# Dealing the tokens to the partitions in two groups, so that the rows of a transfer lie closer together in HBM

## The chip, the core and the metric

The kernel runs on one core of one Trainium2 chip; the other seven cores are idle. The metric is the device time of the whole program in microseconds. Before the change the median of 3 runs is 240.83 us (240.64 to 241.17). The profile is one more execution of the same program: 240.54 us by the clock that the metric uses, and a span of 238.8 us from the first to the last instruction in the trace.

## The reference

Each of 16 x 1024 = 16,384 tokens is a row of 512 float32 numbers (2 KB). It is written out twice, each time multiplied by one of its two weights. The expert indices are an input, but nothing is computed from them.

```python
def setup_inputs():
    batch, seq, hidden, n_experts = 16, 1024, 512, 8
    k = 2
    return {
        "x": np.random.randn(batch, seq, hidden).astype(np.float32),
        "expert_indices": ...,                      # not used
        "expert_weights": np.random.randn(batch, seq, k).astype(np.float32),
    }

def reference(x, expert_indices, expert_weights):
    x_expanded = x[:, :, np.newaxis, :].repeat(k, axis=2)
    weights = expert_weights[..., np.newaxis]
    return (x_expanded * weights).astype(np.float32)   # (16, 1024, 2, 512)
```

So 33.6 MB are read and 67.1 MB are written, for one multiplication per number written.

## The kernel before

Every partition of the on-chip memory gets 128 consecutive tokens (`A_TOTAL`): partition p has the tokens 128p to 128p + 127. One transfer moves, for each of the 128 partitions, one contiguous row of bytes; the rows of one transfer start 128 tokens apart in HBM, which is 256 KB in `x` and 512 KB in `out`.

```python
A_TOTAL = ntok // P                     # 16384 / 128 = 128 tokens per partition
xr = x.rearrange("b s h -> (b s) h").rearrange("(p a) h -> p (a h)", a=A_TOTAL)
outr = ...                              # the same for out, 1024 numbers per token
wr = ...                                # the same for the weights, 2 per token
row = k * hidden                        # 1024 numbers: both copies of a token
TX = 16                                 # tokens per partition in one load
TO = 8                                  # tokens per partition in one store
w_pool = ...(bufs=1); x_pool = ...(bufs=2); o_pool = ...(bufs=4)

w_tile = w_pool.tile([P, A_TOTAL * k], f32)
nc.sync.dma_start(out=w_tile, in_=wr)                       # all weights, once

for i in range(A_TOTAL // TX):                              # 8 loads
    x_tile = x_pool.tile([P, TX * hidden], f32)
    nc.scalar.dma_start(out=x_tile, in_=xr[:, i*TX*hidden : (i+1)*TX*hidden])
    for j in range(TX // TO):                               # 2 stores per load
        o_tile = o_pool.tile([P, TO * row], f32)
        for t in range(TO):
            for kk in range(k):
                nc.vector.tensor_scalar(                    # 128 x 512, times a weight
                    out=o_tile[:, o : o + hidden],
                    in0=x_tile[:, at : at + hidden],
                    scalar1=w_tile[:, c : c + 1], scalar2=None,
                    op0=mybir.AluOpType.mult)
        nc.sync.dma_start(out=outr[:, first : first + TO*row], in_=o_tile)
```

Loads are issued from ScalarE's queue, the weights and the stores from SyncE's queue. A load row is 16 tokens or 32 KB, a store row 8 tokens of two copies or 32 KB; so every load and every store moves 128 rows of 32 KB, 4 MB. There are two buffers for loads and four for stores.

Of the kernel before, what the change touches and what calls it, by code (L numbers as in the profile page):

```python
# [1 line left out]

# [4 lines left out]


@with_exitstack
def kernel(  # L10
    ctx: ExitStack,
    tc: tile.TileContext,
    x: bass.AP,
    expert_indices: bass.AP,
    expert_weights: bass.AP,
    out: bass.AP,
):
    nc = tc.nc

    batch, seq, hidden = x.shape  # L20
    k = expert_weights.shape[-1]
    P = nc.NUM_PARTITIONS
    ntok = batch * seq
    assert ntok % P == 0
    A_TOTAL = ntok // P

    xr = x.rearrange("b s h -> (b s) h").rearrange("(p a) h -> p (a h)", a=A_TOTAL)
    outr = out.rearrange("b s k h -> (b s) (k h)").rearrange(
        "(p a) n -> p (a n)", a=A_TOTAL
    )  # L30
    wr = expert_weights.rearrange("b s k -> (b s) k").rearrange(
        "(p a) k -> p (a k)", a=A_TOTAL
    )
    f32 = mybir.dt.float32
    row = k * hidden

    TX = 16
    TO = 8

    w_pool = ctx.enter_context(tc.tile_pool(name="w_pool", bufs=1))  # L40
    x_pool = ctx.enter_context(tc.tile_pool(name="x_pool", bufs=2))
    o_pool = ctx.enter_context(tc.tile_pool(name="o_pool", bufs=4))

    w_tile = w_pool.tile([P, A_TOTAL * k], f32)
    nc.sync.dma_start(out=w_tile, in_=wr)

    for i in range(A_TOTAL // TX):
        x_tile = x_pool.tile([P, TX * hidden], f32)
        nc.scalar.dma_start(
            out=x_tile, in_=xr[:, i * TX * hidden : (i + 1) * TX * hidden]  # L50
        )
        for j in range(TX // TO):
            o_tile = o_pool.tile([P, TO * row], f32)
            for t in range(TO):
                at = (j * TO + t) * hidden
                for kk in range(k):
                    c = (i * TX + j * TO + t) * k + kk
                    o = t * row + kk * hidden
                    nc.vector.tensor_scalar(  # L59
                        out=o_tile[:, o : o + hidden],  # L60
                        in0=x_tile[:, at : at + hidden],
                        scalar1=w_tile[:, c : c + 1],
                        scalar2=None,
                        op0=mybir.AluOpType.mult,
                    )
            first = (i * TX + j * TO) * row
            nc.sync.dma_start(out=outr[:, first : first + TO * row], in_=o_tile)


# [1 line left out]
_INS = ['x', 'expert_indices', 'expert_weights']  # L71
_OUTS = [((16, 1024, 2, 512), 'float32')]


# [23 lines left out]
```

## Time and profile before

| what | value |
|---|---|
| time, median of 3 | 240.83 us |
| span of the profiled execution | 238.8 us |
| HBM read and written in it | 33.69 MB and 67.11 MB |
| VectorE multiplications | 256, 102.5 us in all |
| loads of `x` | 8 of 4 MB |
| stores of `out` | 16 of 4 MB |
| load of the weights | 1 of 128 KB, landed 10.1 us after its issue |

To read such a profile: the core has 16 DMA engines, and every transfer is spread over them, row by row. "DMA share" is the mean busy share of the 16; a share slightly over 1 comes from packets being counted in the stretch in which they start. "Landing" is the moment when the semaphore of a transfer has its full count, so that an engine waiting for it can go on. "Idle before" of a group of instructions says how long their engine stood still ahead of them, and what ended it; that costs time only if the engine sets the pace.

### The profile page before, as it was taken

What the parts mean: (1) busy time and instruction counts of PE and PEld (TensorE: products, weight loads), DVE (VectorE), ACT (ScalarE), POOL (GpSimd) and SP (SyncE); (2) the same over time, 40 slices, a digit from 0 to 9 for tenths busy, and PEclk for the clock granted to TensorE, in tenths of its full rate; (3) what the DMA queues carried; (4) which work ended last, traced back from release to release, by engine and by line L of the source; (5) the groups of instructions that cost most, each with busy time, mean ns of one, the idle gap of its engine ahead of it and who ended that gap; (6) DMA issues with size and microseconds to landing.
All of it is one profiled execution on the core that took longest, in us unless ns stands there. A gap on an engine that the chain in (4) does not pass through costs nothing.

```text
span 238.8 us, 358 instructions
## 1 busy us (share of the span) xinstructions
DVE 102.5 (43%) x256; POOL 0.2 (0%) x4
## 2 busy tenths in 40 slices
DVE  0079994059701904682054910739008486400000
POOL 0000000000000000000000000000000000000000
DMA  7999999999999999999999999999999999999994
GB/s 277 447 439 417 434 380 417 439 439 439 423 423 428 439 423 412 439 439 439 439 439 434 434 439 439 412 435 428 428 423 434 434 439 439 439 439 434 434 439 214
DMA packets 3602, 100.81 MB, mean 422 GB/s; under 512 B 400, under 2 KB 528, under 8 KB 528
## 3 DMA queue, kind: packets, MB, share of 16 engines
q1 hardware_dynamic: 2448, 67.24, 65.4%
q10 hardware_dynamic: 1152, 33.55, 33.2%
q14 instruction: 2, 0.02, 0.0%
HBM read 33.69 MB, written 67.11 MB: 422 GB/s over the span
## 4 chain that ended last, share of the span: by engine, by line
DMA 62%; DVE 18%; another core or an unknown queue 5%; DVEq 0%; issue 0%
DMA out_dram<-o_tile 57%; DVE o_tile L59 18%; DMA x_tile<-in_x_dram 5%; DVEq L93 0%; DVEq L59 0%
## 5 line engine op out<-in xcount | busy, mean ns | idle before, releaser
L59 DVE TENSOR_SCALAR o_tile<-x_tile,w_tile 128x512 f32<-128x512 f32 x256 | 102.5, 480 | 103.3 <-DMA out_dram<-o_tile 74.1
L82 POOL MEMSET const-bfloat16-1.0<- 128x1 bf16 x1 | 0.1, 101 | 0.0
L82 POOL MEMSET const-uint8-127<- 128x1 uint8 x1 | 0.1, 101 | 0.0
L82 POOL MEMSET const-float32-0.0<- 128x1 f32 x1 | 0.1, 98 | 0.2 <-issue 0.2
L82 POOL MEMSET const-float32-1.0<- 128x1 f32 x1 | 0.1, 98 | 0.0
## 6 DMA issues: line engine op xcount, KB each, us to landing
out_dram<-o_tile SPq DMA_DIRECT2D x16, 4096.0 KB, 44.9
x_tile<-in_x_dram ACTq DMA_DIRECT2D x8, 4096.0 KB, 23.9
w_tile<-in_expert_weights_dram SPq DMA_DIRECT2D x1, 128.0 KB, 10.1
```

The lines of the kernel that those rows point to most:

```text
L59: nc.vector.tensor_scalar(out=o_tile[:, o : o + hidden], in0=x_tile[:, at : at + hidden], scalar1=w_tile[:, c : c + 1], scalar2=None, op0= ...
L82: nc = _bacc.Bacc("TRN2", target_bir_lowering=False, num_devices=1)
```

## The change

The tokens are dealt in two groups. The first group has 65 tokens per partition (tokens 0 to 8,319), the second 63 (the rest). In the first group the rows of a transfer start 65 tokens apart: 130 KB in `x`, 260 KB in `out`. In the second they start 63 tokens apart: 126 KB and 252 KB. The aim is that the rows which the DMA engines work on at the same moment do not all lie at a multiple of 256 KB from one another.

As 65 and 63 don't divide by 16, the loads have other sizes: five loads of 13 tokens (26 KB per row) in the first group, and loads of 16, 16, 16 and 15 tokens in the second. Stores still take at most 8 tokens. A load of 13 tokens is stored as 8 and 5 (rows of 32 and 20 KB), the load of 15 as 8 and 7. The weights come by two transfers, one for each group, into two column ranges of the same tile. The buffers, the multiplications and the queues stay as they are.

```diff
-    xr = x.rearrange("b s h -> (b s) h").rearrange("(p a) h -> p (a h)", a=A_TOTAL)
-    outr = ...
-    wr = ...
+    groups = [[[13], [13], [13], [13], [13]], [[16], [16], [16], [15]]]
...
-    nc.sync.dma_start(out=w_tile, in_=wr)
+    def rows(of_all, done, T):
+        return of_all[done * P : (done + T) * P, :].rearrange(
+            "(p a) n -> p (a n)", a=T
+        )
+    for group in groups:
+        T = sum(sum(t) for t in group)
+        nc.sync.dma_start(
+            out=w_tile[:, done * k : (done + T) * k], in_=rows(wf, done, T)
+        )
+        done += T
...
-    for i in range(A_TOTAL // TX):
+    for group in groups:
+        T = sum(sum(t) for t in group)
+        xr = rows(xf, done, T)
+        outr = rows(of, done, T)
+        a0 = 0
+        for pieces in group:
+            x_tile = x_pool.tile([P, TX * hidden], f32)
+            for n in pieces:
+                nc.scalar.dma_start(
+                    out=x_tile[:, at * hidden : (at + n) * hidden],
+                    in_=xr[:, (a0 + at) * hidden : (a0 + at + n) * hidden],
+                )
...
+            for t in range(at):
+                if t % TO == 0:
+                    o_tile = o_pool.tile([P, TO * row], f32)
...             (the two multiplications of a token, as before)
+                if t + 1 in ends or (t + 1) % TO == 0:
+                    nc.sync.dma_start(
+                        out=outr[:, (a0 + first) * row : (a0 + t + 1) * row],
+                        in_=o_tile[:, first % TO * row : (t % TO + 1) * row],
+                    )
+                    first = t + 1
+            a0 += at
+        done += T
```

More of the change, by code (lines that the diff above doesn't have):

```diff
@@ L25 @@
     A_TOTAL = ntok // P
-    xr = x.rearrange("b s h -> (b s) h").rearrange("(p a) h -> p (a h)", a=A_TOTAL)
[L28 to L33, printed above, removed]
     f32 = mybir.dt.float32
@@ L38 @@
     TO = 8
+    groups = [[[13], [13], [13], [13], [13]], [[16], [16], [16], [15]]]
+    assert sum(sum(sum(t) for t in g) for g in groups) == A_TOTAL
+    xf = x.rearrange("b s h -> (b s) h")
+    of = out.rearrange("b s k h -> (b s) (k h)")
+    wf = expert_weights.rearrange("b s k -> (b s) k")
     w_pool = ctx.enter_context(tc.tile_pool(name="w_pool", bufs=1))
@@ L44 @@
     w_tile = w_pool.tile([P, A_TOTAL * k], f32)
-    nc.sync.dma_start(out=w_tile, in_=wr)
-    for i in range(A_TOTAL // TX):
-        x_tile = x_pool.tile([P, TX * hidden], f32)
-        nc.scalar.dma_start(
-            out=x_tile, in_=xr[:, i * TX * hidden : (i + 1) * TX * hidden]
-        )
[L52 to L55, printed above, removed]
+    def rows(of_all, done, T):
+        return of_all[done * P : (done + T) * P, :].rearrange(
+            "(p a) n -> p (a n)", a=T
+        )
+    done = 0
+    for group in groups:
[4 more added lines that the diff above has]
+        done += T
+    done = 0
+    for group in groups:
[5 more added lines that the diff above has]
+            x_tile = x_pool.tile([P, TX * hidden], f32)
+            at = 0
+            for n in pieces:
[3 more added lines that the diff above has]
+                )
+                at += n
+            ends = [sum(pieces[: i + 1]) for i in range(len(pieces))]
+            first = 0
+            for t in range(at):
+                if t % TO == 0:
+                    o_tile = o_pool.tile([P, TO * row], f32)
                 for kk in range(k):
-                    c = (i * TX + j * TO + t) * k + kk
-                    o = t * row + kk * hidden
+                    c = (done + a0 + t) * k + kk
+                    o = t % TO * row + kk * hidden
                     nc.vector.tensor_scalar(
                         out=o_tile[:, o : o + hidden],
-                        in0=x_tile[:, at : at + hidden],
+                        in0=x_tile[:, t * hidden : (t + 1) * hidden],
                         scalar1=w_tile[:, c : c + 1],
@@ L65 @@
                     )
-            first = (i * TX + j * TO) * row
-            nc.sync.dma_start(out=outr[:, first : first + TO * row], in_=o_tile)
+                if t + 1 in ends or (t + 1) % TO == 0:
[6 more added lines that the diff above has]
+        done += T
 _INS = ['x', 'expert_indices', 'expert_weights']
```

## The prediction

> **What bounds the kernel now.** I read the page first, for who is busy.
>
> ```profile
> span 238.8 us, 358 instructions
> DVE 102.5 (43%) x256; POOL 0.2 (0%) x4
> DMA  7999999999999999999999999999999999999994
> GB/s 277 447 439 417 434 380 417 439 439 439 423 423 428 439 423 412 439 439 439 439 439 434 434 439 439 412 435 428 428 423 434 434 439 439 439 439 434 434 439 214
> ...
> q1 hardware_dynamic: 2448, 67.24, 65.4%
> q10 hardware_dynamic: 1152, 33.55, 33.2%
> ...
> DMA 62%; DVE 18%; another core or an unknown queue 5%; DVEq 0%; issue 0%
> ...
> L59 DVE TENSOR_SCALAR o_tile<-x_tile,w_tile 128x512 f32<-128x512 f32 x256 | 102.5, 480 | 103.3 <-DMA out_dram<-o_tile 74.1
> ```
>
> VectorE works for 43% of the span and stands still for 103.3 us, mostly until a store has emptied a buffer. The 16 DMA engines are busy in every slice but the first and the last: the stores' queue (q1) and the loads' queue (q10) take 65.4 + 33.2 = 98.6% of all engine time. So the kernel is bound by the DMA engines, and the question is whether they move bytes at their best rate. For that I read the table of stretches, where the sixth column is the DMA share and the last the rate:
>
> ```profile
> 0.00:24.00 24.00, 10.69 (x27) 0.20 (x4) 1.00 0.95 393
> 24.00:48.00 24.00, 14.74 (x38) 0.00 (x0) 1.00 1.00 417
> 48.00:96.00 48.00, 22.54 (x57) 0.00 (x0) 1.00 1.01 436
> 96.00:144.00 48.00, 22.43 (x56) 0.00 (x0) 1.00 0.99 427
> 144.00:192.00 48.00, 21.58 (x54) 0.00 (x0) 1.00 1.01 435
> 192.00:234.00 42.00, 10.54 (x27) 0.00 (x0) 1.00 1.01 435
> ```
>
> 435 GB/s is reached with loads and stores mixed (48 to 96, 144 to 192 us) and with stores alone (192 to 234 us, in which only q1 has packets). That is the same figure in three stretches with the rows at the old distance. Only two stretches fall short of it after the start: 24 to 48 us lacks 18 of 435, which is 1.0 us, and 96 to 144 us lacks 8 of 435, 0.9 us. In 0 to 24 us the shortfall is 42 of 435 or 2.3 us, of which about 2.0 are the wait for the first data (the single packet records start at 1.7 us, and the table by 2 us has 11 GB/s up to 2 us). Lost inside the stream: 0.3 + 1.0 + 0.9 = 2.2 us.
>
> The packet records say the same more finely. A row of 32 KB is one packet. Of 3,072 such packets the shortest and the median took 1,213 ns. 69 took over 1,270 ns, and 64 of those are load packets, most of them at 2 us, 21 us and 28 to 38 us from the start, up to 2,505 ns. Their excess over 1,213 ns is 25.5 us of engine time, 1.6 us on each of 16 engines. The page agrees: q1 moved 67.24 MB in 65.4% of 238.8 us, 430.5 GB/s, and q10 33.55 MB in 33.2%, 423 GB/s. At q1's rate the loads would have taken 77.9 us rather than 79.3, 1.4 us less.
>
> The end: the last packet of the fastest engine ends at 235.9 us, of the slowest at 237.6, on average at 236.6. The spread is what the slow packets left behind, and the slowest engine sets the time. The program ends 1.1 us later.
>
> **What the Trainium skill says.** All three places are on the page "DMA: Bandwidth & Descriptors". Its section "Latency and other measured facts" reports that copies from HBM to HBM with a row pitch of 512 KiB ran at 207 GB/s, and at 214 in the best case, and far lower from 2 MiB on; it calls the aliasing of HBM channels an inference. That is the idea of the change. The trace does not show such a loss in steady state: the stores, whose rows lie 512 KB apart, ran at 435 GB/s. Its section "Where 436 GB/s comes from" puts the ceiling of the on-chip ports at 435.2 GB/s. The trace agrees: 435 and 436 in the undisturbed stretches, and the last four stores land 9.68 us apart, 433 GB/s. Its section "Queues, rings and completion order" says that each engine takes turns between its queues packet by packet. The trace agrees: the 128 KB of weights needed 10.1 us to land, as each of an engine's eight 1 KB packets stands between two 32 KB packets of the first load, 1.25 us apart.
>
> **The change part by part.**
>
> *Bytes and multiplications* are the same: 100.8 MB, and 256 x 480 ns on VectorE, off the path.
>
> *Row distance.* At best all slow packets go. The mean engine gains 1.6 us, and the engine that ends last gains that and what it lost more than the mean, 237.6 - 236.6 = 1.0 us: 2.6 us, about 1.1% of the time. The change can't gain more here, since the other 3,003 packets already take the shortest time. I don't expect all of it. The slow packets stand at moments when all engines start on a stream together (the first load, the third and fourth load among the first stores), and rarely in the mixed stream from 48 us on, which has the same row distance. So the row distance is at most half of the cause; the other half would be the starting itself, which stays. I take half: -1.3 us.
>
> *More rows.* 9 loads instead of 8 and 18 stores instead of 16 are 3 x 128 = 384 more packets, the second weights transfer 128: 32 more for each engine. A packet of 1,024 bytes took 44 ns, one of 32,768 bytes 1,213 ns; the line through both has 6.3 ns at zero bytes. 32 x 6.3 ns = 0.2 us. Four more completions per engine at 9 ns (as recorded) add 0.04 us. Together +0.2 us.
>
> *The beginning.* Now the first load lands at 13.3 us. VectorE needs 16 multiplications for the first store, 19.77 - 13.31 = 6.46 us, and by the weights transfer (issued at 0.73, first packet at 1.73 us) the first packet follows 1.0 us after the issue: the store is ready at 20.8 us. The packets of loads 1 and 2 run out at 22.2 us on the first engine and 23.7 us on the last. So no engine stood still. Afterwards a load has 13/16 of the bytes. Each of its eight packets per engine shrinks from 1,213 to about 987 ns, 1.8 us per load. The first load lands at 11.5 us, the store is ready at 19.0 us, and the two loads run out at 18.6 to 20.1 us. The fastest engines wait 0.4 us, the slowest don't. If the slow packets vanish, the loads run out some 0.5 us earlier, and the wait becomes 0.4 to 0.9 us on every engine. I take +0.3 us.
>
> *The middle.* Stores of 5 tokens make the four output buffers hold 26 tokens instead of 32. VectorE waits for the oldest, while three remain queued: at least 5 + 8 + 5 = 18 tokens, 9.4 MB or 21.7 us of transfer at 435 GB/s. It needs 6.4 us to fill the next. The engines don't run dry. *The end* is again a stretch of stores alone, so nothing new.
>
> Sum: 240.8 - 1.3 + 0.2 + 0.3 = 240.0 us. The two dealings have unlike rows on the engines' hands, so the spread at the end may shrink beyond the half that I took; for this I shade to 239.8 us.
>
> **The rivals.** *First, the row distance is the whole cause of the slow packets.* For it: the loads suffer, whose rows are 256 KB apart, and all engines work in step at those moments. Against it: the same distance costs nothing from 48 to 96 us. Then -2.6 + 0.2 + 0.6 gives 239.0 us, and with a little luck in the beginning 238.5. *Second, it is no cause.* The slow packets would be the cost of starting reads, or of writes and reads changing over. Then +0.2 + 0.3 gives 241.3 us. *Third, a new wait on the weights.* The second weights transfer stands behind the first on the same queue and takes turns with the second load: it lands near 18 us. If the first multiplication waited for the whole tile, not for the columns it reads, VectorE would begin at about 18.5 us instead of 11.5, and the first store would be ready at 26 us with the loads gone at 19: seven idle microseconds, 247 us. I think it unlikely (one in twenty-five), as the two transfers write separate columns. *Fourth, the rows of 26 and 20 KB could be cut into more packets, or read less well.* No packet in the trace speaks of it; 1% of the time would already be 2.4 us.
>
> **Range and chances.** To be faster by 2% the time must fall below 236.0. The 100.8 MB alone take 232 us at 435 GB/s; with 1.7 us before the first packet, 1.1 us after the last and the 2 us by which the metric exceeds the span that is 236.8. So this is next to excluded: 0.02. Slower by 2% is over 245.6, by the third or fourth rival: 0.05. Within 2%: 0.93. I give the first rival a third, the half-way case a third, the second rival a quarter. The range that holds these, 238.4 to 241.6 us, should do in 8 of 10 cases.
>
> **What would show the steps right or wrong.** In the profile after: 435 to 437 GB/s in the stretches without a slow packet, no more (else the ceiling was the rows' distance after all, and my main step is wrong). q10's rate from section 3: 430 GB/s if the distance was the cause, 423 if not, and in between as I expect. 24 to 48 us: 435 for the first rival, 417 for the second. First multiplication at 11.5 us (about 18.5 for the third rival), first store issued at 17.9. VectorE's idle time stays near 100 us, still ended by stores. If the rate in the mixed stretches falls below 430, new collisions or cut rows have come, and the prediction fails upward.

## The result: 2.4% slower

The changed kernel takes 246.94 us (median of 6 runs, 245.55 to 248.2), the kernel before 240.95 us beside it (240.64 to 242.0). The ratio is 1.0244, with a 95% interval of 1.0206 to 1.0283. The runs also lie further apart than before: 2.65 us instead of 1.4.

The page of the changed kernel, its counterparts to the lines shown of before:

```profile
span 245.8 us, 368 instructions
...
DVE 102.6 (42%) x256; POOL 0.2 (0%) x4
...
DMA  7999999999999999999999999999999999999961
GB/s 287 424 420 427 373 394 421 456 412 447 405 425 449 469 405 426 434 442 376 421 455 428 432 421 439 430 412 384 472 420 431 427 437 427 427 427 453 422 295 56
...
q1 hardware_dynamic: 2880, 67.24, 64.6%
q10 hardware_dynamic: 1296, 33.56, 32.1%
...
L83 DVE TENSOR_SCALAR o_tile<-x_tile,w_tile 128x512 f32<-128x512 f32 x256 | 102.6, 482 | 110.4 <-DMA out_dram<-o_tile 84.2
```

The reader is to see three things. VectorE has the same work, and it still stands idle for stores. The DMA engines are busy in every slice but the first and the last two. And in this execution it is the stores that move more slowly: q1 had 67.24 MB in 64.6% of 245.8 us, 423.5 GB/s (430.5 before), while q10 had 33.56 MB in 32.1%, 425.3 GB/s (423 before). That is 2.6 us more of mean engine time for the stores and 0.4 us less for the loads.

The table of stretches of the changed kernel (DMA share and GB/s last) says where:

```profile
20.00:31.00 11.00, 11.00 (x29) 0.00 (x0) 1.00 0.97 375
31.00:107.00 76.00, 31.41 (x79) 0.00 (x0) 1.00 1.01 433
107.00:120.00 13.00, 3.53 (x10) 0.00 (x0) 1.00 0.99 408
120.00:160.00 40.00, 20.25 (x51) 0.00 (x0) 1.00 0.99 426
160.00:172.00 12.00, 3.61 (x10) 0.00 (x0) 1.00 0.99 408
172.00:234.00 62.00, 24.17 (x61) 0.00 (x0) 1.00 1.01 437
```

In 138 of these 214 us the stream has its old rate of 433 to 437 GB/s, and from 120 to 160 us it has 426. It falls further in three short stretches, although the engines are nearly as busy as ever (a share of 0.97 to 0.99). The packet records show what is in them: single packets that take longer. Counting packets over 5% above the usual time of their length, there were 69 before, 5 of them of stores; now there are 152, 73 of them of stores. 17 take between 1.9 and 2.1 times the usual time (1 before): five rows of 32 KB at 26.4 us take 2.40 to 2.41 us instead of 1.213, rows of 20 KB at 111.6 to 113.3 us take 1.50 to 1.52 us instead of 0.761, rows of 32 KB at 165 to 168 us up to 2.43 us. The excess of all 152 over the usual times is 54.5 us of engine time, 3.4 us on each of 16 engines, where it was 25.5 and 1.6 us.

That is most of what the average engine ends later, 238.8 instead of 236.6 us. But the span of the profile became 7.0 us longer (the median time 6.0). The rest is in the last stretches, first of the kernel before:

```profile
234.00:236.00 2.00, 0.00 (x0) 0.00 (x0) 1.00 0.72 311
236.00:238.00 2.00, 0.00 (x0) 0.00 (x0) 1.00 0.16 66
238.00:240.00 2.00, 0.00 (x0) 0.00 (x0) 1.00 0.00 0
```

and of the changed kernel:

```profile
234.00:236.00 2.00, 0.00 (x0) 0.00 (x0) 1.00 1.03 446
236.00:238.00 2.00, 0.00 (x0) 0.00 (x0) 1.00 0.27 115
238.00:240.00 2.00, 0.00 (x0) 0.00 (x0) 1.00 0.33 143
240.00:242.00 2.00, 0.00 (x0) 0.00 (x0) 1.00 0.33 143
242.00:244.00 2.00, 0.00 (x0) 0.00 (x0) 1.00 0.07 29
```

A DMA share of 0.33 from 238 to 242 us is five of sixteen engines. The completion records of the last store, one from each engine, say it exactly: eleven engines are done between 236.9 and 237.1 us, and five between 242.3 and 244.4. Before, all sixteen were done between 235.9 and 237.6 us. So the first engine ends 1.0 us later, and the last one 6.8 us later. No engine takes over the rows of one that has fallen behind: from 237.1 us on eleven have no packet any more, while five still have rows. So the slowest engine sets the time.

The lag grows by steps. From the first to the last engine, the first store's completions lie 0.3 us apart (32.2 to 32.5 us), the fifth's 3.9 us (85.0 to 88.9), the seventh's 6.6 us (110.4 to 117.0), and those of each of the last five stores 7.5 us (before: 1.7).

The three weak stretches above (20 to 31, 107 to 120 and 160 to 172 us) do not have the same rows on the engines. The last row of 26 KB begins at 73.7 us and the last of 20 KB at 153.6 us. So from 20 to 31 us there are loads of 26 KB rows; from 107 to 120 us the loads have rows of 32 KB and the stores rows of 32 and 20 KB; and from 160 to 172 us all stores have rows of 32 KB, beside loads of 32 and 30 KB.

### The profile page after: what moved, and what is told of

The parts are those of the page before. It is cut to its first block, busy times and chain, and to the rows that moved or that the text cites. A ratio compares the mean times of both kernels' runs of the same rounds, so it can differ in the third digit from the quotient of the medians.

```text
span 245.8 us, 368 instructions
## 1 busy us (share of the span) xinstructions
DVE 102.6 (42%) x256; POOL 0.2 (0%) x4
## 3 DMA queue, kind: packets, MB, share of 16 engines
q1 hardware_dynamic: 2880, 67.24, 64.6%
q10 hardware_dynamic: 1296, 33.56, 32.1%
## 4 chain that ended last, share of the span: by engine, by line
DMA 71%; DVE 15%; issue 0%; DVEq 0%
DMA out_dram<-o_tile 58%; DVE o_tile L83 15%; DMA x_tile<-in_x_dram 13%; DVEq L123 0%; DVEq L83 0%
## 5 line engine op out<-in xcount | busy, mean ns | idle before, releaser
L83 DVE TENSOR_SCALAR o_tile<-x_tile,w_tile 128x512 f32<-128x512 f32 x256 | 102.6, 482 | 110.4 <-DMA out_dram<-o_tile 84.2
## 6 DMA issues: line engine op xcount, KB each, us to landing
w_tile<-in_expert_weights_dram SPq DMA_DIRECT2D x1, 63.0 KB, 15.3
```

Source lines behind the costliest of these rows:

```text
L83: nc.vector.tensor_scalar(out=o_tile[:, o : o + hidden], in0=x_tile[:, t * hidden : (t + 1) * hidden], scalar1=w_tile[:, c : c + 1], scala ...
```

## The experiments

Theories before the first runs: the **distance** theory (at 130 and 126 KB the engines meet at the same places of HBM), the **size** theory (rows of 26, 32 and 20 KB, which came with the change, put the engines out of step) and the **group** theory (two groups and two weights transfers). The runs fell on several chips of the same kind, whose times for the kernel before differ, so each ratio is to the kernel before on the same chip. The quotient of the two medians differs from it by up to 0.5% (e3_128_13: 247.06 / 242.58 = 1.0185, g6_12_84: 245.44 / 243.49 = 1.0080); e3, f3, g3, g6 and h3 have only 4 runs each. "Ends" are the first and the last completion of the last store in the profile, in us.

| run | what | us | ratio (interval) | ends |
|---|---|---|---|---|
| e1_64_64 | 64+64 tokens, 32 KB rows | 241.05 | 0.9953 (0.9931 to 0.9975) | 236.1, 237.4 |
| e2_80_48 | 80+48, 32 KB rows | 240.72 | 0.9927 (0.9908 to 0.9946) | 236.4, 237.5 |
| e3_128_13 | old distance, 13 as 8+5 | 247.06 | 1.0221 (1.014 to 1.0302) | 238.2, 242.8 |
| e4_65_63_16 | 65+63, 32 KB rows | 240.88 | 0.9928 (0.9906 to 0.9949) | 236.1, 237.7 |
| f1_14_77 | old distance, 14 as 7+7 | 243.81 | 1.0045 (1.0021 to 1.0069) | 237.9, 242.4 |
| f2_16_853 | old distance, 16 as 8+5+3 | 242.22 | 0.9972 (0.9959 to 0.9986) | 237.0, 239.3 |
| f3_16_8 | old distance, loads 16, 8 | 247.57 | 1.0197 (1.0152 to 1.0242) | 242.7, 244.7 |
| c1_before_w2 | before, weights in two | 243.07 | 0.9995 (0.9979 to 1.001) | 235.9, 240.2 |
| g2_13_x3 | 13 as 8+5, 3 load buffers | 244.82 | 1.0068 (1.0045 to 1.009) | 237.4, 240.1 |
| g3_16_then_13 | two loads of 16, then 13 | 247.71 | 1.0208 (1.0145 to 1.0271) | 238.1, 242.9 |
| g4_13_then_16 | two loads of 13, then 16 | 243.67 | 1.0024 (1.0011 to 1.0038) | 237.8, 241.0 |
| g5_12_66 | old distance, 12 as 6+6 | 243.84 | 1.0044 (1.0018 to 1.007) | 237.5, 240.0 |
| g6_12_84 | old distance, 12 as 8+4 | 245.44 | 1.0134 (1.0079 to 1.019) | 239.3, 242.4 |
| h1_after_x3 | 65+63, 13 as 8+5, 3 load buffers | 244.94 | 1.0077 (1.0047 to 1.0107) | 236.5, 242.3 |
| h2_65_63_equal | 65+63, 14 as 7+7 | 243.96 | 1.0004 (0.9964 to 1.0045) | 237.1, 240.9 |
| h3_after_again | changed kernel | 246.79 | 1.0182 (1.0133 to 1.023) | 237.2, 243.4 |
| k1_80_48_again | 80+48, 32 KB rows | 240.77 | 0.9916 (0.989 to 0.9942) | 236.3, 238.1 |
| k2_before_profile | before | 243.57 | 1.0008 (0.999 to 1.0026) | 236.9, 240.8 |

### Distance or size: four runs

The changed kernel with other groups: distances that are powers of two and distances that are not, both with rows of 32 KB; then the old distance with the new lengths, and the new distances with the old lengths:

```diff
-    groups = [[[13], [13], [13], [13], [13]], [[16], [16], [16], [15]]]
+    groups = [[[16]] * 4, [[16]] * 4]                  # e1_64_64
+    groups = [[[16]] * 5, [[16]] * 3]                  # e2_80_48
+    groups = [[[13]] * 9 + [[11]]]                     # e3_128_13
+    groups = [[[16], [16], [16], [16], [1]],
+              [[16], [16], [16], [15]]]                # e4_65_63_16
```

> Two groups of 64 and 64 tokens, all rows 32 KB as before, rows 128 KB apart in x and 256 KB in out; two weights transfers. Distance theory (rows 130 and 126 KB apart let several DMA engines meet at the same place of HBM, so that packets take twice their time and those engines end 5 to 7 us after the others; powers of two do not): as before, 240 to 242 us, packets of 1,213 ns, all engines done within 2 us. Size theory (unequal rows of 26, 20 and 32 KB put the engines out of step): as before too, 240 to 242. Group theory (the two groups and the second weights transfer cost it): 245 to 248 us.

> Two groups of 80 and 48 tokens, all rows 32 KB as before, rows 160 and 96 KB apart in x (320 and 192 KB in out), no power of two. Distance theory: slower than before, 243 to 248 us, with store packets of up to 2,426 ns and a few engines ending over 3 us after the rest. Size theory: as before, 240 to 242 us. Group theory: 245 to 248 us.

> One group of 128 tokens with the old distance of 256 KB, but loads of 13 tokens (nine, then one of 11) and stores of 8 and 5 (last 8 and 3), so rows of 26, 32 and 20 KB. Distance theory: as before, 240 to 242 us, plus some 0.3 us for the additional packets. Size theory: 245 to 248 us with engines ending over 5 us apart. Group theory: as before.

> The new distances (groups of 65 and 63), but loads of 16 tokens and stores of 8 as before, but for one load of 1 token and its store of 1 token at the end of the first group and a last load of 15. Distance theory: 245 to 248 us, some engines over 5 us late. Size theory: 240 to 242.5 us. Group theory: 245 to 248 us.

Measured: 241.05, 240.72, 247.06 and 240.88 us. The distance theory falls with e2_80_48 and e4_65_63_16, the group theory with e1_64_64. The size theory had all four times right: the whole loss comes with the row lengths, at the old distance as well. (The engines of e3_128_13 end 4.6 us apart, where it had over 5.) Side by side, first the new lengths at the old distance (e3_128_13), then the old lengths at the new distances (e4_65_63_16):

```profile
span 244.0 us, 374 instructions
...
GB/s 282 429 428 430 354 369 438 448 450 415 412 432 434 431 412 440 447 402 401 417 451 412 442 408 467 397 446 425 425 426 414 445 440 415 445 414 449 432 415 90
...
q1 hardware_dynamic: 3024, 67.24, 64.8%
```

```profile
span 239.1 us, 365 instructions
...
GB/s 272 444 447 417 428 385 428 439 433 439 433 376 463 444 439 439 433 433 422 439 406 417 439 432 441 433 438 424 426 434 433 433 439 439 439 439 439 439 410 221
...
q1 hardware_dynamic: 2736, 67.24, 65.3%
```

The first has weak slices up to the end and a last slice of 90 GB/s, in which mostly the late engines work. In the second the weakest slices are one of the beginning (385) and one near 70 us (376), where the load of a single token leaves little read ahead; and its last slice has 221.

The shorter distances with old lengths were even below the kernel before. As they share the split of the weights, that could be the reason (c1_before_w2, below).

### Which lengths: unlike rows, or short loads

From here the kernels name the stores of each load as well, which the loops then follow:

```diff
-    groups = [[[13], ...]]
+    groups = [[(14, [7, 7])] * 9 + [(2, [2])]]         # f1_14_77, TO stays 8
+    groups = [[(16, [8, 5, 3])] * 8]                   # f2_16_853
+    groups = [[(16, [8, 8]), (8, [8])] * 5 + [(8, [8])]]   # f3_16_8
+    groups = [[(16, [8, 8])] * 8]                      # c1_before_w2:
+    # weights of tokens 0 to 63 of each partition, then those of 64 to 127
```

> One group, old distance of 256 KB. Loads of 14 tokens (28 KB rows), each stored as 7 and 7 (28 KB rows); a last load and store of 2. So all rows of the stream are equal, but not 32 KB. If rows of unlike lengths are what puts engines behind: as before, 240 to 242.5 us, engines done within 2.5 us of each other. If any row other than 32 KB does it: 245 us or more.

> One group, old distance, loads of 16 tokens as before (32 KB rows), but each stored as 8, 5 and 3 (rows of 32, 20 and 12 KB). If unlike stores suffice: 244 to 248 us, engines ending over 4 us apart. If the shorter loads of 13 tokens are needed for it: 240 to 243 us, with 0.3 us for the 1,024 more packets.

> One group, old distance, all stores of 8 tokens as before (32 KB rows), but loads of 16 and 8 tokens in turn (rows of 32 and 16 KB). If unlike stores are needed: 240 to 242.5 us. If unlike rows of any kind suffice, loads too: 243 to 248 us, engines ending over 3 us apart.

> The kernel before, but with the weights in two transfers (columns of tokens 0 to 63, then 64 to 127). The runs with the shorter distances were 0.5 to 0.7% below the kernel before on their chip; if that came from the distance, this one is equal to the kernel before (ratio 0.998 to 1.002); if from the weights' two transfers, it is 0.993 to 0.995.

f1_14_77: equal rows of 28 KB cost 0.4%, a fifth of what 13 as 8 and 5 cost. In time this is near the first expectation; but in the profiled run, the slowest of its 20 (245.49 us), the engines end 4.5 us apart, which it had excluded, and the excess is 3.4 us on the mean engine, as in the changed kernel. So slow packets and late engines come with equal rows too. What differs is how far it goes: the fastest of the four runs of e3_128_13 takes 245.75 us, though on another chip. f2_16_853: rows of 32, 20 and 12 KB in the stores cost nothing beside loads of 16. So unlike stores do not suffice.

f3_16_8 answers another question than the one asked. Its page:

```profile
DMA  7977999999999999999999999999999999999994
GB/s 280 428 336 320 378 332 437 432 440 410 429 410 448 394 416 432 437 421 432 432 424 426 434 410 426 428 413 456 421 432 432 426 410 453 432 432 432 432 426 208
```

Two loads of 16 and 8 tokens are read before the first store is ready; then the engines have little to do. The third to the sixth slice lack some 94, 110, 52 and 98 of 430 GB/s, over 6.15 us each: 5.1 us, where the kernel before lacks about 1 us in the same slices of its first page. From 15 to 22 us alone the packet records leave the mean engine without a packet for 3.5 us (before: 0.01). That is most of the 2%, and it is a dry start rather than lagging engines, which end only 2.0 us apart. The run tells nothing of unlike rows. c1_before_w2 is the kernel before in time, so the split of the weights is not what made the shorter distances faster.

### Beginning or stream, and read-ahead

```diff
+    groups = [[(13, [8, 5])] * 9 + [(11, [8, 3])]]     # g2_13_x3, with
-    x_pool = ctx.enter_context(tc.tile_pool(name="x_pool", bufs=2))
+    x_pool = ctx.enter_context(tc.tile_pool(name="x_pool", bufs=3))   # TX = 13
+    groups = [[(16, [8, 8])] * 2 + [(13, [8, 5])] * 7 + [(5, [5])]]   # g3_16_then_13
+    groups = [[(13, [8, 5])] * 2 + [(16, [8, 8])] * 6 + [(6, [6])]]   # g4_13_then_16
+    groups = [[(12, [6, 6])] * 10 + [(8, [6, 2])]]     # g5_12_66
```

> One group, old distance, loads of 13 tokens stored as 8 and 5 (the run that was 2.2% slower than before), but with three load buffers instead of two. If the cause is that two short loads hold too few bytes ahead, so that the load queue runs empty more often and starts again: back to 240 to 243 us. If unlike rows alone do it: 245 to 248 us.

> One group, old distance: two loads of 16 first, then seven of 13 stored as 8 and 5, and one of 5. If the loss arises where the first stores meet the third load (a matter of the beginning): as before, 240 to 243 us. If it arises all along the stream of loads of 13: 244 to 247 us.

> One group, old distance: two loads of 13 stored as 8 and 5 first, then six loads of 16 stored as 8 and 8, one of 6. If the loss is a matter of the beginning: 244 to 248 us. If it arises all along the stream of loads of 13: 241 to 243 us.

> One group, old distance: loads of 12 tokens, each stored as 6 and 6, so that all rows of the stream are 24 KB. If unlike rows put the engines out of step, and short loads alone do not: 241 to 243.5 us. If short loads do it, with only 24 tokens read ahead: 246 us or more, worse than with 13.

g3_16_then_13 has the whole loss with an unaltered beginning (1.0208), g4_13_then_16 a tenth of it with the beginning of the changed kernel (1.0024). So the loss is not a matter of the beginning; it comes with the stream of loads of 13. In the profile of g3_16_then_13 the slow packets are mostly loads (51.4 of 60.8 us of excess), in that of the changed kernel mostly stores (38.7 of 54.5). g5_12_66 has still shorter loads and only 24 tokens read ahead, but equal rows: 1.0044. So short loads alone do not do it. g2_13_x3 has the unlike rows and a third buffer: 1.0068, between its two expectations. So the buffer takes away about two thirds of the loss and not all.

### The same remedies at the new distances

```diff
+    groups = [[(12, [8, 4])] * 10 + [(8, [8])]]        # g6_12_84
+    groups = [[(13, [8, 5])] * 5, [(13, [8, 5])] * 4 + [(11, [8, 3])]]
+    # h1_after_x3, with three load buffers of 13 tokens
+    groups = [[(14, [7, 7])] * 4 + [(9, [7, 2])],
+              [(14, [7, 7])] * 4 + [(7, [7])]]         # h2_65_63_equal
+    # h3_after_again: the changed kernel, unaltered
```

> One group, old distance: loads of 12 tokens stored as 8 and 4 (rows of 24, 32 and 16 KB). It differs from the run with 12 stored as 6 and 6 (0.4% slower than before) in nothing but the split of the stores. If unlike rows are one of two conditions of the loss (the other: only two short loads ahead): 246 to 249 us, 1.3% or more above before. If it is the lengths of 26 and 20 KB in particular: 242 to 244.5 us.

> The changed kernel (65 and 63 tokens, the new distances) with loads of 13 throughout (the last of 11) and three load buffers instead of two. If the third buffer gives back what it gave at the old distance, and the shorter distance is worth its 0.5 to 0.7% besides: 0.997 to 1.003 of before, 241.5 to 243.5 us on a chip where before has 242.5. If the distances make the unlike rows worse: above 1.01.

> The groups of 65 and 63 tokens with two load buffers, but loads of 14 stored as 7 and 7 (all rows of the stream 28 KB; at the ends of the groups a load of 9, stored as 7 and 2, and one of 7). If unlike rows were the cause: 0.995 to 1.003 of before. If the short loads are: above 1.01.

> The changed kernel, unaltered, beside the three others on one chip: 1.015 to 1.028 of before, some engines ending 4 to 8 us after the first.

On one chip, the changed kernel is at 1.0182. With equal rows of 28 KB, two buffers and the same 65 and 63 tokens it is at 1.0004; three of these ten runs (244.64 to 245.44 us) count as slow and are left out of the ratio, and the quotient of the medians of all runs is 1.0019. With unlike rows and three buffers it is at 1.0077, more than expected: the shorter distance gave nothing on top of the buffer. g6_12_84 is 0.9% above g5_12_66 by the ratios and 0.5% by the medians, on two chips. That it is above was expected if unlike rows matter, but not all of it is theirs. Its first store waits for 8 tokens instead of 6, with little read ahead. First g5_12_66, then g6_12_84:

```profile
GB/s 272 423 436 432 293 428 436 433 428 432 424 432 440 416 432 416 436 436 420 432 436 432 412 436 442 424 436 436 416 444 424 440 418 443 428 428 448 428 418 232
```

```profile
GB/s 275 433 347 431 366 398 433 459 412 432 437 449 436 382 431 425 414 427 427 444 401 409 444 436 392 417 458 412 420 428 447 398 436 447 409 452 428 431 439 199
```

From the third to the sixth slice g5_12_66 lacks 0, 4, 143 and 8 of 436 GB/s over 6.0 us each, 2.1 us in all, and g6_12_84 lacks 89, 5, 70 and 38 over 6.1 us, 2.8 us. So 0.7 us of the difference, 0.3%, belong to the beginning; the 0.2 to 0.6% that remain are what the split of the stores can have cost.

### The distance alone

> Groups of 80 and 48 tokens with all rows of 32 KB (the run that was 0.7% faster than before), once more with more rounds: if its gain is real, 0.991 to 0.997 of before, and the engines end within 2 us of each other. If it was that chip's doing, 0.998 to 1.002.

> The kernel before, unaltered, for its profile on the same chip as the run with 80 and 48 tokens. If the old distance of 256 KB leaves some engines behind on this chip, they end over 3 us after the first here, and within 2 us with 80 and 48 tokens; if the spreads are alike, the distance has no part in the difference.

With 80 and 48 tokens and rows of 32 KB the time is 240.77 us, 0.9916 of before. Stretches of that kernel,

```profile
144.00:192.00 48.00, 21.12 (x53) 0.00 (x0) 1.00 1.01 434
236.00:238.00 2.00, 0.00 (x0) 0.00 (x0) 1.00 0.16 66
238.00:240.00 2.00, 0.00 (x0) 0.00 (x0) 1.00 0.00 0
```

and of the kernel before on the same chip:

```profile
144.00:192.00 48.00, 19.27 (x48) 0.00 (x0) 1.00 1.00 424
236.00:238.00 2.00, 0.00 (x0) 0.00 (x0) 1.00 0.46 197
238.00:240.00 2.00, 0.00 (x0) 0.00 (x0) 1.00 0.27 115
```

Here the old distance has more slow packets within the stream and leaves engines behind as well: they end 236.9 to 240.8 us, with 3.0 us of excess on the mean engine, against 236.3 to 238.1 us and 1.6 us. The average engine ends 1.5 us later (238.3 against 236.8), and the last is 2.5 us behind the average instead of 1.3. The profiled run of the kernel before, at 243.72 us, lies near the median of its 20 (243.57). In its first profile the kernel before had neither (1.7 us apart, 1.6 us of excess), and took 240.95 us in the comparison with the changed kernel; which chip that was is not known, so 80 and 48 tokens may never have run on it. So the aim of the change was sound, and a kernel that beats both here is there: 80 and 48 tokens, all rows of 32 KB. On the two chips where it was run it is worth 0.7 and 0.8%; by the first profile it may be worth less elsewhere.

## Why the prediction was wrong

**The bound, the stores and the beginning: right.** The DMA engines remained the bound, and none of the long stretches exceeded 437 GB/s. The first multiplication began at 11.36 us (11.5 predicted), the first store was issued at 17.81 us (18.0 by the prediction: 11.5 + 6.46). The 0.3 us for engines that wait for the first store did not come: from 15 to 22 us the mean engine is without a packet for 0.06 us. VectorE did not wait for the second weights transfer, which landed 15.3 us after its issue; the third rival is refuted.

**The row distance: wrong in its reasoning.** I gave the slow load packets of the first 38 us half to the distance, and took 1.3 us off. They do not depend on it. The runs with rows of 32 KB at 128, 160 and 96, and 130 and 126 KB have 28.1, 26.8 and 25.9 us of excess, nearly all of it before 42 us; the kernel before has 25.5. Where the distance counted (k1_80_48_again against k2_before_profile), it was with slow packets later in the stream and with engines left behind, which the one profile that I had did not show.

**More rows: the step that failed.** "More rows" charged the new lengths with 6.3 ns for each additional packet, 0.2 us in all, and "The middle" only asked whether the engines would run dry. No run shows the 6.3 ns to be wrong, and the engines did not run dry: from 4 to 235 us the mean engine is without a packet for 0.13 us in all. Missing was that with the new lengths, while the engines are busy, more packets take longer, and some engines get far more of that than others. The trace shows 1.8 us more excess on the mean engine (3.4 against 1.6). The average engine ends 2.2 us later, and the last is 5.6 us behind the average (1.0 before): 2.2 + 4.6 make the 6.8 us. That the lengths are the reason is shown by e3_128_13 (1.0221 with them at the old distance) and e4_65_63_16 (0.9928 without them at the new). I had read the spread at the end as a remainder that could only shrink ("the spread at the end may shrink beyond the half"). It was the quantity to ask for.

**The fourth rival was the nearest.** It had rows of 26 and 20 KB being read less well, but I gave it no mechanism and little weight. Nor is it quite that: a row of 20 KB takes 0.761 us, its proper time, in all but 9 of 640 cases.

**What is shown, and what is open.** Shown: the loss comes with the lengths and not with the distance or the groups; it does not come from the beginning; in the profile of the changed kernel a third of it is the average engine and two thirds the engines that end last. Equal rows take nearly all of it away at the new distances (1.0004, or 1.0019 by all runs), and a third load buffer, with loads of 13 throughout, more than half. Unlike stores beside loads of 16 cost nothing (f2_16_853), equal rows with short loads under 0.5% (f1_14_77, g5_12_66); so neither alone makes the loss.

Not shown is that unlike rows and short loads must meet. The one pair in which the split of the stores alone differs, g5_12_66 and g6_12_84, leaves 0.2 to 0.6% for it and not 2%; loads of 14 stored as 8 and 6 were not tried. In the changed kernel two of the three weak stretches come after the last row of 26 KB, and in one of them all stores have rows of 32 KB. And such slow packets and late engines are there with equal rows too, in the profiles of f1_14_77 (3.4 us of excess) and of k2_before_profile (3.0 us). Argued only: with equal rows an engine that is one packet behind does the same kind of packet in the same slot as the others, with unlike rows it does not, and where a new load starts beside running stores such engines collide. Open: what the slowed engines share when their packets take twice as long. No packet record names its engine.

## What to carry to other kernels

Where transfers are the bound, read not only the rate of the stream but also how far apart the engines complete the last transfer: here no engine took over the rows of another, and the slowest set the time. When a change of layout brings new row lengths, test the lengths and the layout apart; here the layout was worth up to 0.8% and the lengths cost 2.2%. Here group sizes that keep all rows of loads and stores at 32 KB were the better choice (80 and 48 instead of 65 and 63).

## What was unexpected of the hardware

Packets took double their time (within some per cent) in some engines only, for one or several in a row, while the others went on at full rate: 2.40 us for 32 KB and 1.51 us for 20 KB. Rows 256 KB apart and rows 160 and 96 KB apart differed by 0.7 and 0.8% on two chips; on the one where both have a profile, about half of that is slow packets within the stream (424 against 434 GB/s from 144 to 192 us) and about half engines left behind. At its best the stream has 435 to 436 GB/s at either distance. And the first reads of the program, and the first load beside stores, are slow at any distance: some 26 us of engine time, 1.6 us of the span.
